# Residues of weights and block sums in the seven-product jobs of a hybrid decoder block on one core

## The chip, the cores and the metric

The kernel runs on one core of one Trainium2 chip. The metric is the device time of one execution in microseconds (us); where several executions are timed, their median. One execution is also recorded by the hardware profiler; its trace gives the start and the length of every instruction.

## What is computed

One decoder block on x of shape (1, 256, 2048), all in float32:

```
h = rms_norm(x);  z = h @ w_in                       # 2048 x 11280, split into p, q, k, v, g, r, gates
y_a = pool_mixer(p) @ w_branch_a                      # trailing-window means
o   = gated linear attention(q, k, v, g), rms_norm, * silu(r)
y_b = o @ w_branch_b
x   = x + rms_norm((sig(g0) * y_a + sig(g1) * y_b) @ w_out)
h   = rms_norm(x)
x   = x + rms_norm((silu(h @ w_ffn_gate) * (h @ w_ffn_up)) @ w_ffn_down)   # 5632 wide
```

Nearly all work is in the products with w_in, w_branch_a, w_branch_b, w_out, w_ffn_gate, w_ffn_up and w_ffn_down: 256 rows of activations against weights that are read once.

## The kernel before, in words

**Precision.** Each float32 operand is held as a high part in TensorE's round float32 type and a low part that is the rest. A product is three matmuls: high activations by high weights, high by low, low by high. For weights, ScalarE writes the high part `wh` and VectorE the low part `wl` (lines 340 and 344, 407 and 411); for activations the tiles are called h0h, h0l and so on.

**Jobs.** The plan (a generator at the top) cuts the weights into jobs of 512 columns. A job's weights come in steps of two blocks of 128 rows (class `Step`): 12 matmuls of 512 columns (lines 371 to 373), weights streaming, activations (128 columns) loaded as the stationary operand. The first jobs (kinds p, q, k) run across: there the weights are stationary and the activations stream, 256 columns (lines 360 to 362).

**The seven products.** 46 jobs are marked fast. Their first eight row blocks are done as a 2 by 2 block product with seven multiplications in place of eight (class `Part`: q1, r5, q6, q7, q2, q4, r3). Each product is 4 row blocks x 3 matmuls = 12 matmuls of 256 columns (lines 431 to 433), weights streaming again. In r5, q7, q6 and r3 the activations are sums or differences of blocks, made once for an activation by `combine` and kept in tiles `x`, `fx` (for the three parts of the FFN product) or `ox` (for o). In q1, q2 and q4 they are blocks of the whole activations. The other row blocks of a fast job are steps: four steps in a job with 16 row blocks, two in one with 12.

**Order.** Jobs are merged by `merged`: in the long run of a product TensorE sees, job after job, q2, a step, q4, q1 of the next job, r3, r5 of the next, a step, q6, a step, q7, a step. Transposes for the next operand (line 203) are put between units by `to_operand` and others. Weights are prepared four units ahead (`prepare_to`), so DMAs, ScalarE and VectorE work ahead of TensorE.

**Where tiles lie.** Each tile has a byte address in every partition. Modulo 256, summed from the tile sizes in order of the pools and the pads of 64 (pool `his`) and 192 bytes (pool `wp`): whole activations, high and low, 0; weights `wh` and `wl` of steps and of the seven products alike, 64, in slots of 4352 = 17 x 256 bytes; block sums `x` 128 (a slot at 0 and AT_X = 128); block sums `fx` 128 (a slot at 64 and AT_F = 64); block sums `ox` 0; raw weights 192 or 64 in turn; blocks of raw weights for the seven products, 64. All steps inside these tiles are multiples of 256 bytes. The text calls the residue of the streaming operand less that of the stationary one, modulo 256, the **relation** of a matmul. It is 64 for steps and for q1, q2, q4; 64 for all seven in the w_branch_b jobs; 192 in r5, q7, q6 and r3 of the others. In the jobs that run across it is 0 - 64 = 192.

Of the kernel before, what the change touches and what calls it, by code (L numbers as in the profile page):

```python
# [8 lines left out]
F32 = mybir.dt.float32  # L9
# [5 lines left out]
P = 128  # L15
# [14 lines left out]
HW = CW // 2  # L30
# [4 lines left out]


LINE = 256
PAD_A, PAD_B, PAD_W = 64, 0, 192
ROOM_W = 4352
AT_X, AT_F = 128, 64  # L40
ROOM_X = 8448
AHEAD = 12
SUMS_AHEAD = 7
# [9 lines left out]
COMBOS = ("r5", "q7", "q6", "r3")  # L53
# [55 lines left out]
def tile_hybrid_block(ctx: ExitStack, tc: tile.TileContext, *aps):  # L109
# [4 lines left out]
    act, dve, pool, pe, sync = nc.scalar, nc.vector, nc.gpsimd, nc.tensor, nc.sync  # L114

    one = ctx.enter_context(tc.tile_pool(name="one", bufs=1))
    his, st, los, rest = [ctx.enter_context(tc.tile_pool(name=n, bufs=b))
                          for n, b in (("his", 1), ("st", 4), ("los", 1), ("rest", 1))]
    wp = ctx.enter_context(tc.tile_pool(name="wp", bufs=BUFS))
# [7 lines left out]
    late = {}  # L127

    def placed(pool, shape, tag, name, lead=0, room=0):

        n = 1
        for k in shape:
            n *= k
        t = pool.tile([P, max(room // 4, n)], F32R, tag=tag, name=name)[:, lead // 4:lead // 4 + n]
        if len(shape) == 2:
            return t.rearrange("p (a b) -> p a b", a=shape[0])
        return t.rearrange("p (a b c) -> p a b c", a=shape[0], b=shape[1])
# [3 lines left out]
    def nm(s):  # L141
        uid[0] += 1
        return f"{s}_{uid[0]}"
# [10 lines left out]
    def f32(ap):  # L154
        return ap.bitcast(F32)


    for p_, n in ((his, PAD_A), (los, PAD_B), (wp, PAD_W)):
        if n:
            p_.tile([P, n // 4], F32, tag="pad", name=nm("pad"), bufs=1)  # L160
    xa = [one.tile([P, D], F32, tag=f"X{t}", name=f"x{t}") for t in range(NT)]
    ident = one.tile([P, P], F32, tag="ident", name="ident")
    masks = two_st.tile([P, 64 * MASKED + P], I32, tag="masks", name="masks")
# [48 lines left out]
    def extra(a):  # L212


        if a.name == "o":
            k = [two_st.tile([P, 2, 4, P], F32R, tag=f"K{i}", name=nm("ox")) for i in range(2)]
            q = [[two_st.tile([P, 4, P], F32R, tag=f"{x}{i}", name=nm("ox")) for i in range(2)] for x in ("Q", "AD")]
            return [tuple(x) for x in q] + [(x[:, 0], x[:, 1]) for x in k]
        if a.name[0] == "f":
            if not late:  # L220
                early.close()
                late["pool"] = ctx.enter_context(tc.tile_pool(name="late", bufs=1, reuse_waits="tile"))
            x = [placed(late["pool"], (len(COMBOS), 4, P), f"fx{i}", nm("fx"), AT_F, ROOM_X) for i in range(2)]
        else:
            x = [placed(pool_, (len(COMBOS), 4, P), f"R{i}", nm("x"), AT_X, ROOM_X) for i, pool_ in enumerate((his, rest))]
        return [(x[0][:, n], x[1][:, n]) for n in range(len(COMBOS))]

    class Act:
# [16 lines left out]
        def combine(self):  # L245

            self.x = {}
            parts = {}
            pieces = extra(self)

            def block(name, g, t):
                parts[name] = scratch().rearrange("p (k c) -> p k c", k=4)
                c = (slice(None), slice(None), slice(t * P, (t + 1) * P))
                dve.tensor_tensor(parts[name], f32(self.hi[g][c]), f32(self.lo[g][c]), op=ALU.add)

            def put(which, name):
                n, src = COMBOS.index(which), parts.pop(name)
                hi, lo = pieces[n]
                act.activation(hi, src, AF.Copy)
                dve.tensor_tensor(lo, src, f32(hi), op=ALU.subtract)  # L260
                self.x[which] = (hi, lo)
                parts[which] = src

            def differ(dst, a, b, op=ALU.subtract):
                dve.tensor_tensor(parts[dst], parts[a], parts[b], op=op)

            return [lambda: (block("21", 0, 1), block("22", 1, 1)),
                    lambda: (differ("22", "21", "22"), put("r5", "22")),
                    lambda: (block("11", 0, 0), differ("21", "11", "21")),
                    lambda: (put("q7", "21"), differ("11", "r5", "11")),  # L270
                    lambda: (put("q6", "11"), block("12", 1, 0)),
                    lambda: (differ("12", "12", "q6", ALU.add), put("r3", "12"))]
# [47 lines left out]
    class Step:  # L320
# [16 lines left out]
        def high(self):  # L337
            self.load()
            self.hi = placed(wp, (GK, self.j.width), "wh", nm("wh"), room=ROOM_W)
            act.activation(self.hi, self.raw, AF.Copy)  # L340

        def low(self):
            self.lo = placed(wp, (GK, self.j.width), "wl", nm("wl"), room=ROOM_W)
            dve.tensor_tensor(self.lo, self.raw, f32(self.hi), op=ALU.subtract)  # L344
# [32 lines left out]
    class Part:  # L377
# [25 lines left out]
                pool.dma_start(self.block((0, 1)), self.block((0, 0)), accum_op=ALU.add)  # L403

        def high(self):
            self.hi = placed(wp, (4, HW), "wh", nm("wh"), room=ROOM_W)
            act.activation(self.hi, self.src, AF.Copy)  # L407

        def low(self):
            self.lo = placed(wp, (4, HW), "wl", nm("wl"), room=ROOM_W)  # L410
            dve.tensor_tensor(self.lo, self.src, f32(self.hi), op=ALU.subtract)  # L411

        def left(self, i):
# [689 lines left out]
```

## Time and profile before

| | |
|---|---|
| median of 3 runs | 1479.87 us (1478.96 to 1480.27) |
| profiled execution, its own time | 1477.55 us |
| span from its first to its last instruction | 1475.7 us |
| TensorE matmul busy | 1454.2 us, 99% |
| VectorE busy | 1219.9 us, 83% |
| ScalarE busy | 907.6 us, 62% |
| granted TensorE clock, mean | 0.999 |

In a timeline row the first number is the start in us from the span's start, the second the length of the instruction. Matmuls overlap (a new one starts while the one before still drains), so a matmul's length says little; the pace is the difference between the starts of two successive ones, and the time of a unit of 12 matmuls is the start of the next unit less its own.

### The profile page before, as it was taken

How to read it: one execution, taken by the hardware profiler on the slowest of the kernel's cores; microseconds unless marked ns; L12 is line 12 of the kernel's file. 1: busy time of each engine (PE TensorE's matmuls, PEld its weight loads, DVE VectorE, ACT ScalarE, POOL GpSimd, SP SyncE). 2: the span in 40 equal slices, each digit the busy share in tenths (PEclk: the TensorE clock that was granted, in tenths of full speed). 3: DMA queues.
4: the chain of work that ended last, by engine and by line, in shares of the span. 5: the costliest groups of instructions: out<-in, count | busy, mean ns of one | idle time of the engine just before them, and what ended most of it. 6: DMA issues, size and time to landing. Idle time of an engine off the chain costs nothing.

```text
span 1475.7 us, 23511 instructions
## 1 busy us (share of the span) xinstructions
PE 1454.2 (99%) x9156; PEld 1299.3 (88%) x9156; DVE 1219.9 (83%) x1359; ACT 907.6 (62%) x1185; POOL 73.0 (5%) x96
## 2 busy tenths in 40 slices
PE   8999999999999999999999999999999999999997
PEld 7988999888888888889878988998998899998886
DVE  6765445789899897799778899888889899889997
ACT  6457433556676665556666666666666666666663
POOL 2000000000110000000000000000000000000001
PEclk9999999999999999999999999999999999999999
DMA  8857765435668688658855677777766777777654
GB/s 286 272 179 230 216 188 182 129 100 184 229 188 258 191 255 259 208 169 283 259 186 158 214 225 220 228 227 230 245 216 212 228 231 228 228 237 229 202 176 144
DMA packets 88896, 314.70 MB, mean 213 GB/s; under 512 B 10140, under 2 KB 10352, under 8 KB 88528
## 3 DMA queue, kind: packets, MB, share of 16 engines
q1 hardware_dynamic: 77616, 279.15, 56.4%
q0 software_dynamic: 8160, 28.59, 10.2%
q10 hardware_dynamic: 3008, 5.45, 1.0%
q8 instruction: 72, 1.18, 0.3%
q14 instruction: 40, 0.33, 0.1%
HBM read 284.84 MB, written 4.19 MB: 196 GB/s over the span
## 4 chain that ended last, share of the span: by engine, by line
PE 85%; DVE 6%; issue 3%; DMA 3%; ACT 2%; POOL 0%; SPq 0%; DVEq 0%; ACTq 0%; POOLq 0%
PE acc L372 15%; PE acc L373 15%; PE acc L371 15%; PE ac L432 5%; PE ac L431 5%; PE ac L433 5%; PE acc L433 4%; PE acc L432 4%; PE acc L431 4%; PE acc L362 3%; PE acc L360 3%; PE acc L361 3%; DVE wl L411 2%; DVE wl L344 2%; PE tr L685 1%
## 5 line engine op out<-in xcount | busy, mean ns | idle before, releaser
L340 ACT ACTIVATE wh<-raw 128x1024 fp32r<-128x1024 f32 (+1 forms) x336 | 355.3, 1059 | 303.3 <-PE acc L373 129.8
L344 DVE TENSOR_TENSOR wl<-raw,wh 128x1024 fp32r<-128x1024 f32 (+1 forms) x336 | 410.5, 1223 | 130.5 <-ACT wh L340 128.0
L411 DVE TENSOR_TENSOR wl<-blocks,wh 128x1024 fp32r<-128x1024 f32 x322 | 390.8, 1222 | 71.6 <-ACT wh L407 69.7
L407 ACT ACTIVATE wh<-blocks 128x1024 fp32r<-128x1024 f32 x322 | 338.5, 1059 | 158.3 <-PE acc L373 65.7
L431 PE MATMUL ac<-wh,x 128*128 128x256 f32 x396 | 110.4, 279 | 0.0
L432 PE MATMUL ac<-wl,x 128*128 128x256 f32 x396 | 109.9, 278 | 0.0
L433 PE MATMUL ac<-wh,x 128*128 128x256 f32 x396 | 109.8, 277 | 0.0
L403 POOL DMA_DIRECT2D blocks<-blocks x46 | 39.9, 867 | 812.9 <-DVE wl L344 209.5
L431 PEld LDWEIGHTS ac<-wh,x 128*128 128x128 f32 x396 | 74.5, 188 | 2.9
L432 PEld LDWEIGHTS ac<-wl,x 128*128 128x128 f32 x396 | 74.4, 188 | 3.1
L433 PEld LDWEIGHTS ac<-wh,x 128*128 128x128 f32 x396 | 74.4, 188 | 0.0
L372 PE MATMUL acc<-wl,h22h 128*128 128x512 f32 x176 | 69.6, 395 | 0.2
L371 PE MATMUL acc<-wh,h22h 128*128 128x512 f32 x176 | 69.4, 394 | 0.2 <-ACT wh L340 0.2
L373 PE MATMUL acc<-wh,h23l 128*128 128x512 f32 x176 | 69.3, 394 | 0.0
L373 PE MATMUL acc<-wh,h22l 128*128 128x512 f32 x176 | 69.2, 394 | 0.0
L372 PE MATMUL acc<-wl,h23h 128*128 128x512 f32 x176 | 69.1, 392 | 0.0
L371 PE MATMUL acc<-wh,h23h 128*128 128x512 f32 x176 | 68.4, 390 | 0.5 <-ACT wh L340 0.5
L396 DVE TENSOR_TENSOR blocks<-blocks,blocks 128x1024 f32<-128x1024 f32 x46 | 56.3, 1223 | 1.3
L392 DVE TENSOR_TENSOR blocks<-blocks,blocks 128x1024 f32<-128x1024 f32 x46 | 56.2, 1221 | 0.7
L394 DVE TENSOR_TENSOR blocks<-blocks 128x1024 f32<-128x1024 f32 x46 | 56.1, 1219 | 0.1
L371 PE MATMUL acc<-wh,h3h 128*128 128x512 f32 (+1 forms) x128 | 49.6, 387 | 0.0
L372 PE MATMUL acc<-wl,h3h 128*128 128x512 f32 (+1 forms) x128 | 49.5, 387 | 0.0
(536 smaller groups left out, 4096.9 us busy)
## 6 DMA issues: line engine op xcount, KB each, us to landing
raw<-in_w_in_dram SPq DMA_DIRECT2D x128, 512.0 KB, 4.1
raw<-in_w_ffn_gate_dram SPq DMA_DIRECT2D x48, 512.0 KB, 4.4
raw<-in_w_ffn_up_dram SPq DMA_DIRECT2D x48, 512.0 KB, 4.4
blocks<-blocks POOLq DMA_DIRECT2D x46, 512.0 KB, 6.1
blocks<-in_w_ffn_down_dram SPq DMA_DIRECT2D x44, 512.0 KB, 4.3
raw<-in_w_ffn_down_dram SPq DMA_DIRECT2D x44, 512.0 KB, 4.4
blocks<-in_w_in_dram SPq DMA_DIRECT2D x40, 512.0 KB, 4.5
blocks<-in_w_ffn_gate_dram SPq DMA_DIRECT2D x40, 512.0 KB, 4.3
```

Source lines behind the costliest of these rows:

```text
L340: act.activation(self.hi, self.raw, AF.Copy)
L344: dve.tensor_tensor(self.lo, self.raw, f32(self.hi), op=ALU.subtract)
L371: pe.matmul(ps, ah, hi[:, i, cs], start=first, stop=False, skip_group_check=j.fast)
L372: pe.matmul(ps, ah, lo[:, i, cs], start=False, stop=False, skip_group_check=j.fast)
L373: pe.matmul(ps, al, hi[:, i, cs], start=False, stop=last, skip_group_check=j.fast)
L392: dve.tensor_tensor(b12, b12, b22, op=ALU.add)
L396: dve.tensor_tensor(b21, b21, b12, op=ALU.add)
L407: act.activation(self.hi, self.src, AF.Copy)
L411: dve.tensor_tensor(self.lo, self.src, f32(self.hi), op=ALU.subtract)
L431: pe.matmul(dst, ah, wh, start=i == 0 and p in ("q1", "r5"), stop=False, skip_group_check=True)
L432: pe.matmul(dst, ah, wl, start=False, stop=False, skip_group_check=True)
L433: pe.matmul(dst, al, wh, start=False, stop=i == 3 and p in EARLY, skip_group_check=True)
```

## The change

The slots and their sizes stay; what lies in them is shifted. The weights of the seven products start 128 bytes further into their slots (residue 192 in place of 64), those of steps stay at 64. The block sums `x` start at their slot's begin (residue 0 in place of 128), `fx` 192 bytes into it (0 in place of 128). `ox` stays at 0. A pad of zero bytes is dropped; it allocated nothing.

```diff
-PAD_A, PAD_B, PAD_W = 64, 0, 192
+PAD_A, PAD_W = 64, 192
 ROOM_W = 4352
-AT_X, AT_F = 128, 64
+LEAD_FAST = 128
+LEAD_F = 192
 ROOM_X = 8448
...
-            x = [placed(late["pool"], (len(COMBOS), 4, P), f"fx{i}", nm("fx"), AT_F, ROOM_X) for i in range(2)]
+            x = [placed(late["pool"], (len(COMBOS), 4, P), f"fx{i}", nm("fx"), LEAD_F, ROOM_X) for i in range(2)]
         else:
-            x = [placed(pool_, (len(COMBOS), 4, P), f"R{i}", nm("x"), AT_X, ROOM_X) for i, pool_ in enumerate((his, rest))]
+            x = [placed(pool_, (len(COMBOS), 4, P), f"R{i}", nm("x"), room=ROOM_X) for i, pool_ in enumerate((his, rest))]
...
         def high(self):
-            self.hi = placed(wp, (4, HW), "wh", nm("wh"), room=ROOM_W)
+            self.hi = placed(wp, (4, HW), "wh", nm("wh"), LEAD_FAST, ROOM_W)
             act.activation(self.hi, self.src, AF.Copy)
 
         def low(self):
-            self.lo = placed(wp, (4, HW), "wl", nm("wl"), room=ROOM_W)
+            self.lo = placed(wp, (4, HW), "wl", nm("wl"), LEAD_FAST, ROOM_W)
             dve.tensor_tensor(self.lo, self.src, f32(self.hi), op=ALU.subtract)
```

The relation becomes 192 in all seven products of every fast job and stays 64 in steps.

## Rows read from the trace of the kernel before

**Rows 1.** From the page: the span, TensorE's busy time, and its granted clock in 40 slices.

```profile
span 1475.7 us, 23511 instructions
PE 1454.2 (99%) x9156; PEld 1299.3 (88%) x9156; DVE 1219.9 (83%) x1359; ACT 907.6 (62%) x1185; POOL 73.0 (5%) x96
...
PEclk9999999999999999999999999999999999999999
```

**Rows 2.** The list of waits of TensorE over the whole span, longest total first (in total, times, longest); its first three.

```profile
PE tr L203 <- DMA x<-in_x_dram: 4.1, 6, 1.2
PE acc L372 <- DVE wl L344: 1.8, 2, 1.5
PE acc L371 <- ACT wh L340: 1.2, 3, 0.6
```

**Rows 3.** From the page's costliest groups: the four groups that write the weights of steps (lines 340, 344) and of the seven products (lines 407, 411); busy us, mean ns of one.

```profile
L340 ACT ACTIVATE wh<-raw 128x1024 fp32r<-128x1024 f32 (+1 forms) x336 | 355.3, 1059 | 303.3 <-PE acc L373 129.8
L344 DVE TENSOR_TENSOR wl<-raw,wh 128x1024 fp32r<-128x1024 f32 (+1 forms) x336 | 410.5, 1223 | 130.5 <-ACT wh L340 128.0
L411 DVE TENSOR_TENSOR wl<-blocks,wh 128x1024 fp32r<-128x1024 f32 x322 | 390.8, 1222 | 71.6 <-ACT wh L407 69.7
L407 ACT ACTIVATE wh<-blocks 128x1024 fp32r<-128x1024 f32 x322 | 338.5, 1059 | 158.3 <-PE acc L373 65.7
```

**Rows 4.** Timeline of TensorE from 924 to 937 us, first matmul of each unit of 12 (line 371 a step, line 431 one of the seven products).

```profile
924.58 0.39 PE L371 MATMUL acc<-wh,h22h 128*128 128x512 f32 x1
...
927.33 0.28 PE L431 MATMUL acc<-wh,h21h 128*128 128x256 f32 x1
...
928.69 0.28 PE L431 MATMUL ac<-wh,f00h 128*128 128x256 f32 x1
...
930.05 0.28 PE L431 MATMUL acc<-wh,x 128*128 128x256 f32 x1
...
932.77 0.39 PE L371 MATMUL acc<-wh,h22h 128*128 128x512 f32 x1
...
935.52 0.28 PE L431 MATMUL ac<-wh,fx 128*128 128x256 f32 x1
...
936.89 0.39 PE L371 MATMUL acc<-wh,h23h 128*128 128x512 f32 x1
```

**Rows 5.** Timeline of TensorE from 948 to 955 us: four transposes, then the first matmul of each unit.

```profile
948.48 0.60 PE L203 MATMUL tr<-ident,scr 128*128 128x128 f32 x4
948.83 0.36 PE L431 MATMUL acc<-wh,f01h 128*128 128x256 f32 x1
...
950.33 0.28 PE L431 MATMUL ac<-wh,f00h 128*128 128x256 f32 x1
...
951.74 0.28 PE L431 MATMUL acc<-wh,fx 128*128 128x256 f32 x1
...
953.12 0.28 PE L431 MATMUL ac<-wh,fx 128*128 128x256 f32 x1
...
954.48 0.39 PE L371 MATMUL acc<-wh,f02h 128*128 128x512 f32 x1
```

**Rows 6.** Timeline of TensorE from 822 to 843 us, first matmul of each unit.

```profile
822.88 0.28 PE L431 MATMUL ac<-wh,h20h 128*128 128x256 f32 x1
...
824.29 0.28 PE L431 MATMUL acc<-wh,x 128*128 128x256 f32 x1
...
825.71 0.28 PE L431 MATMUL ac<-wh,x 128*128 128x256 f32 x1
...
827.12 0.40 PE L371 MATMUL acc<-wh,h22h 128*128 128x512 f32 x1
...
829.93 0.28 PE L431 MATMUL ac<-wh,x 128*128 128x256 f32 x1
...
831.34 0.40 PE L371 MATMUL acc<-wh,h23h 128*128 128x512 f32 x1
...
834.15 0.28 PE L431 MATMUL ac<-wh,x 128*128 128x256 f32 x1
...
838.36 0.28 PE L431 MATMUL acc<-wh,h21h 128*128 128x256 f32 x1
...
839.78 0.40 PE L371 MATMUL acc<-wh,h22h 128*128 128x512 f32 x1
...
842.54 0.28 PE L431 MATMUL acc<-wh,h21h 128*128 128x256 f32 x1
```

**Rows 7.** Busy time of TensorE by stretch, 158 to 247 us, when nothing but matmuls of jobs that run across is on it (length, busy and, in brackets, the number of matmuls; then the granted clock).

```profile
158.00:247.00 89.00, 89.00 (x758) 1.00 0.65 197
```

**Rows 8.** Timeline of TensorE: the first and the last of the 81 products among the 322 whose matmuls ran at 117 to 119 ns from start to start, each by its second and its fourth group of three (the last is followed by the step behind it).

```profile
330.08 0.28 PE L431 MATMUL ac<-wh,h0h 128*128 128x256 f32 x1
...
330.79 0.28 PE L431 MATMUL ac<-wh,h0h 128*128 128x256 f32 x1
...
1440.67 0.28 PE L431 MATMUL acc<-wh,f21h 128*128 128x256 f32 x1
...
1441.38 0.28 PE L431 MATMUL acc<-wh,f21h 128*128 128x256 f32 x1
...
1441.73 0.40 PE L371 MATMUL acc<-wh,f22h 128*128 128x512 f32 x1
```

**Rows 9.** Timeline of TensorE: the second and the third product after the transposes at 863.68 us, first matmul of each.

```profile
865.48 0.28 PE L431 MATMUL ac<-wh,h20h 128*128 128x256 f32 x1
...
866.84 0.28 PE L431 MATMUL acc<-wh,x 128*128 128x256 f32 x1
```

More of the change, by code (lines that the diff above doesn't have):

```diff
@@ L155, in f32 @@
         return ap.bitcast(F32)
-    for p_, n in ((his, PAD_A), (los, PAD_B), (wp, PAD_W)):
-        if n:
-            p_.tile([P, n // 4], F32, tag="pad", name=nm("pad"), bufs=1)
+    for p_, n in ((his, PAD_A), (wp, PAD_W)):
+        p_.tile([P, n // 4], F32, tag="pad", name=nm("pad"), bufs=1)
     xa = [one.tile([P, D], F32, tag=f"X{t}", name=f"x{t}") for t in range(NT)]
```

## The prediction

> **What bounds the kernel now.** I read the page's first two parts, then the waits of TensorE, then the timeline unit by unit. TensorE is busy for 1454.2 of 1475.7 us, and every slice of the span shows the granted clock at its upper level, 2.4 GHz [rows 1]. Its three longest waits add up to 7.1 us [rows 2]. So TensorE is the bound nearly everywhere, and only two things can move the end: the number of matmuls, which the change leaves as it is, and the pace at which one matmul follows another.
>
> The pace is where the reader has to look closely, because lengths of matmuls hide it. A product of 12 matmuls of 256 columns takes 1.36 us from its first start to the next unit's (927.33 to 928.69), that is 113 ns a matmul; a step takes 2.75 us (924.58 to 927.33) [rows 4]. But the same product can take more. After four transposes the products at 948.83 and 950.33 take 1.50 and 1.41 us, and the next two, on block sums, 1.38 and 1.36 [rows 5]. In [rows 6] products take 1.41 or 1.42 us one after the other, steps between them 2.81 us (827.12 to 829.93 and 831.34 to 834.15), and the quick pace is back only at 842.54. Clock and operands are alike in both. I read this as **two paces** of the same matmuls: 113 ns (quick) and 118 ns (slow, 0.71 us for six in [rows 8]). Going through all 322 products in this way, 81 ran slow, the first at 329.62 and the last at 1440.32 us; [rows 8] shows both at that pace.
>
> Three things about the paces matter for the change.
> - Transposes between units tend to leave the slow pace behind [rows 5], though not always: in [rows 9] the product after such a set is quick, 1.36 us.
> - With a constant relation of the two operands the slow pace does not heal. In the jobs that run across, 758 matmuls fill 89 us, 117 ns each, without a return to 113 [rows 7].
> - With a change of relation it may heal. In [rows 5] the slow pace ends where products on whole activations (relation 64) give way to products on block sums (relation 192); in [rows 6], at 824.29, the same change does nothing. Counted over the timeline in the same way, this meeting of a slow product of relation 64 with one of 192 occurs 15 times: 9 heal (one in [rows 5]), 6 do not (one in [rows 6]).
>
> **The change, part by part.**
>
> *Removed and added instructions:* none. No DMA, no wait and no queue is touched, and slots keep their sizes, so no other tile moves.
>
> *Writers of the shifted tiles.* ScalarE needs 1059 ns for a `wh`, whether it reads raw weights at residue 192 or 64 or blocks at 64; VectorE needs 1223 and 1222 ns for a `wl` in the two cases [rows 3]. No row shows a `wh` at 192, but source residues that differ by 128 make no difference here, so I take 0. Should each write cost 10 ns more, 322 of them would be 3 us per engine, and both engines idle far longer than that in front of these lines, waiting for others [rows 3]; what covers them is TensorE's own length. In this part the range gets nothing.
>
> *Products on block sums (r5, q7, q6, r3).* Both operands move by 128, the relation stays at 192. If only the relation counts, their own pace is unchanged.
>
> *Products on whole activations (q1, q2, q4, and all seven on `ox`).* Their relation goes from 64 to 192. Both relations run at 113 ns when quick: 1.36 us for the whole ones at 927.33 and 928.69, 1.36 us each for the two on block sums from 930.05 to 932.77 [rows 4]. So the steady quick pace costs 0.
>
> *Entry behind a step.* A product that keeps the step's relation takes 1.36 us behind it (927.33), one that changes it takes 1.37 us (935.52 to 936.89) [rows 4]: 0.01 us. There are 83 products of relation 64 straight behind a step in the trace, and all change their relation now: 83 x 0.01 = **+0.8 us**. From below, if a shift of the streaming operand is free where one of the loaded operand was not, the 84 entries that pay today pay nothing: -0.8 us.
>
> *Healing.* This is the large term. The order behind a set of transposes is q4, q1, r3, r5, step, q6, step, q7, step. Today the relation changes between q1 and r3, two products after the transposes. Afterwards it is 192 for all four, and changes only at steps (192 to 64 and back). That is the pattern of [rows 6] from 824.29 on, where products at 192 and steps at 64 alternate and both stay slow over four products and three steps; the pace is quick again only after a product of relation 64 has had its turn, at 842.54. No such product is left after the change. Prices: 1.41 - 1.36 = 0.05 us a product, 2.805 - 2.75 = 0.055 us a step.
>
> How much of the kernel would that catch, if a slow pace once set held until the next set of transposes that leaves a quick one? From 812 us on, eight sets leave it slow (821, 907, 949, 1115, 1158, 1200, 1324, 1407 us) and three quick (864, 1073, 1367). Between a slow one and the next quick one lie 2 + 8 + 12 + 3 = 25 jobs: 175 products, of which 35 are slow already, 140 x 0.05 = 7.0 us; 100 steps, of which 4 are slow already, 96 x 0.055 = 5.3 us. Before 812 us, the stretches 456 to 617 and 684 to 770 us hold about 53 quick products and 36 quick steps that follow a slow spell: 2.7 + 2.0 us. Together **17.0 us** at full persistence. From below the term can be negative: if the new residues prevent the slow pace, all of today's goes, 81 x 0.05 + 16 x 0.055 = 4.9 us.
>
> Between these ends I take the share in which a change of relation failed to heal, 6 of 15: 0.4 x 17.0 = **+6.8 us**.
>
> *Sum:* +0.8 + 6.8 = +7.6 us. Against the profiled execution, 1477.55 us, that gives 1485.2 us. That execution lies 2.3 us under the median of the runs shown; on the median, 1479.87 us, the forecast is **1487.5 us**.
>
> A rule that speaks against any effect: the same step and the same product have two times in the rows above, and the relation changes at places where the pace changes. The Trainium skill, "TensorE: Matmul & The Clock Gate", section "Step-by-step: what each phase is for", says that TensorE reads SBUF through two independent ports, so that loading the next stationary operand takes nothing from the running matmul. By it residues would be of no account and the sum 0 us.
>
> **The rivals.**
> - *B, healing at steps.* The slow pace ends at the first step behind the transposes, since the relation now changes there, so two more products per slow set are slow: 14 sets x 2 x 0.05 = 1.4 us, with the entries at most +2.2 us, at least about 0: 1480 to 1482 us, centre 1481. For it: 9 of 15 changes of relation healed. Against it: in [rows 6] three steps healed nothing. Residues without any effect, the case of the cited rule, give the same within 0.2%.
> - *C, the other side: no slow pace left.* Its place is the first product behind a set of transposes. If weights at 192 against activations at 0 fall into the quick pace there, as one set in [rows 9] did with weights at 64, nothing sets the slow pace and 4.9 us go: 1475.0 us. It decides if more than 3 of the 4.9 us go, that is if about 6 in 10 slow spells vanish. Against it: the jobs that run across stay slow at this very relation [rows 7].
> - *D, slow throughout.* 241 quick products and 162 quick steps of fast jobs turn slow: 12.1 + 8.9 = 21 us, 1501 us. Against it: some sets leave the quick pace [rows 9], and [rows 4] shows quick alternation of 192 and 64.
>
> **How the numbers follow.** The forecast case (slow pace that outlives most steps) has 0.41; its own range is 1482.9 to 1497.7 us, from a fifth of the persistence term to all of it. B has 0.31, C 0.24, D 0.04. The predicted time is the forecast's, 1487.5 us. The range must reach to B and C: 1475.0 to 1496.0 us leaves out D, the uppermost end of the forecast and the part of C that gains all. A change of 0.2%, 3 us, is about what a measurement of this kernel can tell. Faster by more: most of C, 0.22. Slower by more: the forecast and D, 0.45. Within: B and the rest of C, 0.33.
>
> **What would show it.** In the changed kernel's timeline, behind transposes such as those before 948.83, q4, q1, r3 and r5 should take 1.41 us each, the step behind them 2.81 and not 2.75, and q6 again 1.41; a set that leaves the quick pace should give 1.36 us up to the next transposes. Every product straight behind a step should take 1.37 us or more. Writers of weights should keep 1059 and 1222 ns, waits of TensorE their few us. Rival B shows as 2.75 us in the first step behind a slow set, rival C as 1.36 us in the second product behind most sets. The forecast is wrong if the slow products number about 81 again, or if the quick pace itself is no longer 113 ns.

## The result, and the profile after

The changed kernel's median is 1485.71 us (1483.37 to 1486.76, 6 runs), that of the kernel before on the same chip 1479.41 us (1475.85 to 1480.27, 6 runs). The ratio is 1.0048, with a 95% interval of 1.0038 to 1.0058: slower by 6 to 7 us, where 7.6 were forecast (1487.5 us). The way to it is another one than forecast.

From the page of the changed kernel: span, TensorE's busy time, granted clock, and the two groups that write the shifted weights (busy us, mean ns of one). They answer to [rows 1, 3].

```profile
span 1483.7 us, 23511 instructions
PE 1463.9 (99%) x9156; PEld 1307.8 (88%) x9156; DVE 1220.3 (82%) x1359; ACT 906.9 (61%) x1185; POOL 72.9 (5%) x96
...
PEclk9999999999999999999999999999999999999999
...
L411 DVE TENSOR_TENSOR wl<-blocks,wh 128x1024 fp32r<-128x1024 f32 x322 | 391.1, 1221 | 74.8 <-ACT wh L407 70.9
...
L407 ACT ACTIVATE wh<-blocks 128x1024 fp32r<-128x1024 f32 x322 | 337.9, 1057 | 157.2 <-PE acc L373 62.7
```

The span is 8.0 us longer and TensorE is busy 9.7 us longer, with as many matmuls and the clock at its upper level in every slice. The writers take 1221 and 1057 ns, against 1222 and 1059 before. TensorE's waits, as in [rows 2] (total, times, longest):

```profile
PE tr L203 <- DMA x<-in_x_dram: 3.1, 5, 1.2
PE acc L372 <- DVE wl L344: 1.8, 3, 1.0
```

They are no longer than before, so the 8 us lie in the pace of the matmuls. The next view is the timeline of TensorE in the changed kernel from 865 to 879 us: four transposes, then the first matmul of each unit (of the first step also the second triple). It answers to [rows 5, 9].

```profile
865.64 0.60 PE L203 MATMUL tr<-ident,scr 128*128 128x128 f32 x4
866.00 0.37 PE L431 MATMUL acc<-wh,h21h 128*128 128x256 f32 x1
...
867.45 0.28 PE L431 MATMUL ac<-wh,h20h 128*128 128x256 f32 x1
...
868.81 0.28 PE L431 MATMUL acc<-wh,x 128*128 128x256 f32 x1
...
870.17 0.28 PE L431 MATMUL ac<-wh,x 128*128 128x256 f32 x1
...
871.53 0.40 PE L371 MATMUL acc<-wh,h22h 128*128 128x512 f32 x1
...
872.23 0.39 PE L371 MATMUL acc<-wh,h22h 128*128 128x512 f32 x1
...
874.29 0.28 PE L431 MATMUL ac<-wh,x 128*128 128x256 f32 x1
...
875.70 0.40 PE L371 MATMUL acc<-wh,h23h 128*128 128x512 f32 x1
...
878.46 0.28 PE L431 MATMUL ac<-wh,x 128*128 128x256 f32 x1
```

Read the differences of the starts. Behind the transposes q4 takes 1.45 us (0.20 us of it between its first two matmuls), and q1, r3 and r5 take 1.36 us each: the quick pace, where [rows 5] had 1.50 and 1.41 for the first two. Then comes a step, 871.53 to 874.29, and the product behind it is slow: 874.29 to 875.70, 1.41 us. The step behind that one takes 2.76 us, not the 2.81 of a slow one. Of the 11 sets of transposes from 812 us on, 6 leave the quick pace like this one (3 before); in the other 5 the first two products are slow, in 4 of them all four, and the first undisturbed step behind those is quick all the same, as at 956.91 (2.76 us), with a slow product behind it (1.42 us):

```profile
955.50 0.28 PE L431 MATMUL ac<-wh,fx 128*128 128x256 f32 x1
...
956.91 0.40 PE L371 MATMUL acc<-wh,f02h 128*128 128x512 f32 x1
...
959.67 0.28 PE L431 MATMUL ac<-wh,fx 128*128 128x256 f32 x1
...
961.09 0.40 PE L371 MATMUL acc<-wh,f03h 128*128 128x512 f32 x1
```

**What the transposes leave no longer matters much: the products' pace is lost at every step, and the steps themselves stay quick.**

Counted in the starts over the whole trace, 268 of 322 products are slow (81 before). Of the 167 products straight behind a step, 166 are slow. Before, 67 of the 83 at relation 64 (whole activations, and six on `ox`) and 70 of the 84 on the other block sums were quick there.

Where the 8 us lie, worked out over all starts of matmuls, from the first to the last:

| spacings between starts of matmuls | before, us | after, us | difference |
|---|---|---|---|
| in products, undisturbed (3833 spacings in either trace) | 439.73 | 448.38 | +8.65 |
| in products, with a stall or transposes | 9.44 | 8.62 | -0.82 |
| in steps, from 325 us on, undisturbed | 636.59 | 638.57 | +1.98 |
| in steps, with a stall | 25.59 | 24.50 | -1.09 |
| in jobs that run across, and the rest | | | -0.75 |
| sum | | | +7.97 |

187 more slow products x 0.05 us make 9.4 us. Before, 70 quick products on block sums paid 0.01 us each behind a step; that is gone, which takes 0.7 us back and gives the 8.65. Steps take 2 us more in sum: a step behind a product takes 2.763 us in the mean, against 2.754 before, when 16 steps of 2.80 us were among them and the others took 2.748. Its first triple now needs 0.70 us (871.53 to 872.23), then it runs as before. The 16 slow steps of before all stand straight behind slow products at 64/128, as in [rows 6]; the change leaves no product with these residues, and but for one step the pace of 2.80 us is gone.

### The profile page after: what moved, and what is told of

It is laid out like the page before. It is cut to its first block, busy times and chain, and to the rows that moved or that the text cites. A ratio compares the mean times of both kernels' runs of the same rounds, so it can differ in the third digit from the quotient of the medians.

```text
span 1483.7 us, 23511 instructions
## 1 busy us (share of the span) xinstructions
PE 1463.9 (99%) x9156; PEld 1307.8 (88%) x9156; DVE 1220.3 (82%) x1359; ACT 906.9 (61%) x1185; POOL 72.9 (5%) x96
## 4 chain that ended last, share of the span: by engine, by line
PE 87%; DVE 5%; issue 3%; DMA 2%; ACT 1%; POOL 0%; SPq 0%; DVEq 0%; ACTq 0%; POOLq 0%
PE acc L371 16%; PE acc L373 15%; PE acc L372 15%; PE ac L431 5%; PE ac L432 5%; PE ac L433 5%; PE acc L431 4%; PE acc L433 4%; PE acc L432 4%; PE acc L362 3%; PE acc L360 3%; PE acc L361 3%; DMA raw<-in_w_in_dram 2%; DVE wl L344 2%; PE tr L685 1%
## 5 line engine op out<-in xcount | busy, mean ns | idle before, releaser
L340 ACT ACTIVATE wh<-raw 128x1024 fp32r<-128x1024 f32 (+1 forms) x336 | 355.1, 1059 | 309.9 <-PE acc L373 130.6
L411 DVE TENSOR_TENSOR wl<-blocks,wh 128x1024 fp32r<-128x1024 f32 x322 | 391.1, 1221 | 74.8 <-ACT wh L407 70.9
L407 ACT ACTIVATE wh<-blocks 128x1024 fp32r<-128x1024 f32 x322 | 337.9, 1057 | 157.2 <-PE acc L373 62.7
L392 DVE TENSOR_TENSOR blocks<-blocks,blocks 128x1024 f32<-128x1024 f32 x46 | 56.2, 1222 | 0.9
L371 PE MATMUL acc<-wh,h2h 128*128 128x512 f32 (+1 forms) x128 | 49.6, 388 | 0.0
```

The source lines that it names most:

```text
L371: pe.matmul(ps, ah, hi[:, i, cs], start=first, stop=False, skip_group_check=j.fast)
L392: dve.tensor_tensor(b12, b12, b22, op=ALU.add)
```

## The experiments

Every experiment keeps instructions, queues, slots and order; only residues differ, always by a multiple of 128 bytes from one of the two kernels. The lines of code are cuts, in 1 to 8 against the changed kernel, in 9 and 10 against the one before. Ratios are against the kernel before on the same chip. "192/0" is a matmul with streaming operand (weights) at residue 192 and stationary one (activations) at 0. "Behind a step" counts products that follow a step directly and undisturbed.

**1. The sums moved alone.** Sums at 0, weights all at 64: every relation is 64.

```diff
-LEAD_FAST = 128
+LEAD_FAST = 0
```

> Half of the change: block sums at residue 0, weights of the products back at 64, so the relation is 64 everywhere and neither operand's residue moves between a step and a product. Theory M (the streaming operand's residue moves from 64 to 192 at the border from a step to a product, and that sets the slow pace): no border is left, so products straight behind a quick step are quick, 1.36 us; slow ones come from transposes alone. Between 60 and 200 slow products of 322, 1476 to 1486 us. Theory R (weights at 192 over activations at 0 are slow behind any step): the same, under 100 slow products, about 1477 us. Theory K (the prediction's: transposes set the slow pace, only a change of relation can heal it): no change of relation is left, over 250 slow products, about 1488 us.

Measured: 1480.32 us, ratio 1.0033 (1.002 to 1.0045); 220 products slow. Timeline of its TensorE, first matmul of each unit:

```profile
869.16 0.39 PE L371 MATMUL acc<-wh,h22h 128*128 128x512 f32 x1
...
871.90 0.28 PE L431 MATMUL ac<-wh,x 128*128 128x256 f32 x1
...
873.32 0.39 PE L371 MATMUL acc<-wh,h23h 128*128 128x512 f32 x1
...
876.06 0.28 PE L431 MATMUL ac<-wh,x 128*128 128x256 f32 x1
```

A slow product (1.42 us) stands between two steps of 2.74 us. With one relation everywhere the slow pace of products lives through quick steps: 60 of 167 products behind steps are quick. This part of the change alone costs 0.33% of the time, the whole change 0.48%. The count lies outside what each of the three theories expected.

**2. The weights moved alone.** Products 192/0 and 192/128.

```diff
-LEAD_F = 192
+LEAD_F = 64
...
-            x = [placed(pool_, (len(COMBOS), 4, P), f"R{i}", nm("x"), room=ROOM_X) ...
+            x = [placed(pool_, (len(COMBOS), 4, P), f"R{i}", nm("x"), 128, ROOM_X) ...
```

> The other half: weights of the products at 192, block sums at 128 as before. The relation is then 64 in the products on block sums, as in steps, and 192 in those on whole activations. Theory M: the streaming operand moves at every border, so nearly all products behind a step are slow, about 268 slow ones, 1486 us as with the whole change. A theory by relation alone (only a change from 64 to 192 at the border counts): of the products behind steps, those on block sums (q6, q7, about half) are quick, 1.36 us, and 120 to 180 are slow, about 1482 us. Theory K: about 81 to 180 slow, 1480 to 1484 us.

Measured: 1481.23 us, 1.0037 (1.0025 to 1.005); 184 slow. Its timeline:

```profile
875.71 0.28 PE L431 MATMUL ac<-wh,x 128*128 128x256 f32 x1
...
877.07 0.40 PE L371 MATMUL acc<-wh,h23h 128*128 128x512 f32 x1
...
879.83 0.28 PE L431 MATMUL acc<-wh,h21h 128*128 128x256 f32 x1
...
881.24 0.40 PE L371 MATMUL acc<-wh,h22h 128*128 128x512 f32 x1
```

The same kernel, both products behind a step of 64/0: on block sums (192/128) 1.36 us, on whole activations (192/0) 1.41 us. Over the trace 81 of 84 of the former are quick and 0 of 83 of the latter. This is the clearest run against my main reading: 192/0 has the very relation, 192, that 64/128 had before the change, where 70 of 84 were quick behind the same steps. So the relation alone does not decide the pace of a product, although the expectation by relation alone comes nearest to this run's counts; both residues count.

**3. All weights at 192**, those of steps too (same two lines as in the change, in class Step: lines 339 and 343).

```diff
-            self.hi = placed(wp, (GK, self.j.width), "wh", nm("wh"), room=ROOM_W)
+            self.hi = placed(wp, (GK, self.j.width), "wh", nm("wh"), LEAD_FAST, ROOM_W)
```

> The change, and the weights of steps moved by 128 bytes too: all weights at 192, all activations at 0, relation 192 everywhere, no border. Theory M: as with the sums moved alone, since nothing moves between step and product: between 60 and 200 slow products, 1476 to 1486 us. Theory R: all products behind steps slow, 260 or more, 1486 us or more. Theory K: constant relation, over 250 slow, about 1488 us.

Measured: 1486.88 us, 1.0077 (1.0063 to 1.0091); only 76 slow. Its timeline:

```profile
873.95 0.28 PE L431 MATMUL ac<-wh,x 128*128 128x256 f32 x1
...
875.31 0.39 PE L371 MATMUL acc<-wh,h22h 128*128 128x512 f32 x1
...
878.10 0.28 PE L431 MATMUL ac<-wh,x 128*128 128x256 f32 x1
...
879.47 0.39 PE L371 MATMUL acc<-wh,h23h 128*128 128x512 f32 x1
```

Products are quick again, 1.36 and 1.37 us (137 of 167 behind steps), now that products and steps lie alike. The time goes to the steps: 2.79 us (875.31 to 878.10), in every undisturbed step from 325 us on. Their undisturbed spacings, counted as in the table above, make 646.7 us against 636.6 before: +10.2 us of the 10.8 measured. Lines 339 and 343 also place the weights of the jobs that run across, whose relation goes from 192 to 64; their matmuls keep 117 ns (117.2 in the mean before, 117.5 here). The count is what theory M expected, the time is not.

**4. The mirror**: steps at 192, products at 64, activations and sums at 0 (experiment 3, with 0 for LEAD_FAST in lines 406 and 410).

> The border mirrored: weights of steps at 192, weights of products at 64, all activations at 0. Theory M: the streaming operand moves by 128 at each border as in the change, only the other way, modulo 256 the same: about 268 slow products, 1486 us. If the direction counts, the products behind steps are quick and the time is 1475 to 1478 us. Theory R: products at 64 over 0, quick behind steps as in the kernel before, under 100 slow, about 1477 us.

Measured: 1495.59 us, 1.0135 (1.0121 to 1.0149), the slowest of all; 317 slow, 1 of 167 quick behind steps. Its timeline:

```profile
875.48 0.28 PE L431 MATMUL ac<-wh,x 128*128 128x256 f32 x1
...
876.90 0.39 PE L371 MATMUL acc<-wh,h22h 128*128 128x512 f32 x1
...
879.69 0.28 PE L431 MATMUL ac<-wh,x 128*128 128x256 f32 x1
```

Products 1.42 us, steps 2.79: here weights that move by 128 bytes between a step and a product over unmoved activations make the product slow from the other side as well, as 64/0 to 192/0 did in the change. None of the three expectations had a time near this.

**5. The kernel before with the products' weights 256 bytes further** (LEAD_FAST = 256, sums at 128 as before).

> The kernel before with the weights of the products 256 bytes further into their slots (residue modulo 256 as before, 64; sums at 128). If residues count modulo 256, nothing changes: about 81 slow products of 322, ratio 0.998 to 1.002. If what counts is that the streaming operand lies elsewhere in its slot, or a modulus of 512 or more, the products straight behind steps turn slow as with 128 bytes: 180 or more slow ones, ratio 1.003 or more.

Measured: 1476.35 us (11 runs), 0.9996 (0.9986 to 1.0005). A whole 256 bytes do nothing that can be told from no change; half of it, over the same sums, gave 1.0037 (experiment 2). So residues modulo 256 count. Its profiled execution had 110 slow products (61 of 83 and 62 of 84 quick behind steps), that of the kernel before 81. I take this for a variation between executions, whose times go from 1474.0 to 1480.0 us for the kernel before on this chip alone; with one trace of each kernel it isn't shown.

**6. The activations moved in place of the weights**: all weights 64, all activations and sums 128 (`ox` 0).

```diff
-PAD_A, PAD_W = 64, 192
+PAD_A, PAD_W = 192, 64
...
-LEAD_FAST = 128
-LEAD_F = 192
+LEAD_FAST = 0
+LEAD_F = 64
```

> All weights at 64 as before, all activations and block sums at 128 (pads changed; only the sums for w_branch_b stay at 0): relation 192 everywhere, reached from the other side than with all weights at 192. If the pace of a step goes by the relation, steps take 2.80 us as they did there and products are mostly quick (under 110 slow): ratio 1.006 to 1.009. If it goes by where the weights lie (64 quick, 192 slow), steps take 2.75 us, and the ratio is 0.997 to 1.004 depending on what transposes leave.

Measured: 1485.87 us, 1.0063 (1.005 to 1.0076); 48 slow. Its timeline:

```profile
872.87 0.28 PE L431 MATMUL ac<-wh,x 128*128 128x256 f32 x1
...
874.23 0.39 PE L371 MATMUL acc<-wh,h22h 128*128 128x512 f32 x1
...
877.02 0.28 PE L431 MATMUL ac<-wh,x 128*128 128x256 f32 x1
```

The picture of experiment 3, and what was expected if a step goes by the relation: quick products (154 of 161 behind steps), steps of 2.79 us. Steps at 64/128 and at 192/0 share nothing but the relation 192; those at 64/0 take 2.75. So for **steps** the relation does count: 0.05 us each between 64 and 192, as far as these three pairs of residues tell; relation 64 was run in steps as 64/0 alone.

**7. Sums and their weights only**: sums' products 192/128, whole ones left at 64/0.

```diff
-            self.hi = placed(wp, (4, HW), "wh", nm("wh"), LEAD_FAST, ROOM_W)
+            self.hi = placed(wp, (4, HW), "wh", nm("wh"), LEAD_FAST * (self.part in COMBOS), ROOM_W)
```

> Products on block sums with weights at 192 and sums at 128, products on whole activations with weights at 64 over 0, steps at 64 over 0: relation 64 everywhere, though both operands move by 128 at the border of a product on sums. Theory S (a relation changed by the streaming operand at the border sets the slow pace; both moved together or nothing moved does not): q6 and q7 behind steps quick, 1.36 us, q2 and q4 quick unless transposes left the slow pace; 60 to 140 slow products, ratio 0.999 to 1.003. If any movement of the streaming operand at a border sets the slow pace, q6 and q7 are slow: 180 or more, ratio 1.004 or more.

Measured: 1483.20 us, 1.0044 (1.0029 to 1.0058); 237 slow. A miss. Its timeline:

```profile
877.78 0.28 PE L431 MATMUL ac<-wh,x 128*128 128x256 f32 x1
...
879.14 0.40 PE L371 MATMUL acc<-wh,h23h 128*128 128x512 f32 x1
...
881.90 0.28 PE L431 MATMUL acc<-wh,h21h 128*128 128x256 f32 x1
...
883.31 0.40 PE L371 MATMUL acc<-wh,h22h 128*128 128x512 f32 x1
```

The sums' products are quick behind steps (80 of 84; 877.78, 1.36 us). The whole ones, which lie exactly as before the change and whose steps do too, are slow: 1 of 77 quick (881.90, 1.41 us). So the step hands on something of the products *before* it.

**8. The mirror with sums at 128**: experiment 3 with the sums of experiment 2; all weights 192, sums' products 192/128.

> All weights at 192, whole activations at 0 (steps, q1, q2, q4: relation 192), block sums at 128 (r5, q7, q6, r3: relation 64): the border of the sums' products is mirrored, and it is the loaded operand that moves. Theory S: these products stay quick behind steps, as in the kernel before, though their relation changes; under 120 slow products, steps 2.80 us as with all weights at 192, ratio 1.006 to 1.009. If any change of relation from 192 to 64 sets the slow pace (as when it was done with the weights, 317 slow), over 180 slow products, ratio 1.010 to 1.014.

Measured: 1490.25 us, 1.0095 (1.008 to 1.011); 133 slow. Its timeline:

```profile
875.08 0.28 PE L431 MATMUL ac<-wh,x 128*128 128x256 f32 x1
...
876.44 0.39 PE L371 MATMUL acc<-wh,h22h 128*128 128x512 f32 x1
...
879.23 0.28 PE L431 MATMUL ac<-wh,x 128*128 128x256 f32 x1
...
880.64 0.40 PE L371 MATMUL acc<-wh,h23h 128*128 128x512 f32 x1
```

The product ahead of the step is quick (1.36 us), that behind it slow (1.41), with the same two residues. Behind steps 82 of 83 products at 192/0 are quick and 0 of 84 at 192/128. My theory by then, that a shift of the loaded operand alone does no harm, falls.

**What orders the runs so far.** The three matmuls of a triple (high by high, high by low, low by high) are not spaced alike. In nanoseconds, the spacings of a quick step are 226, 229 and 232, in this order in the kernel before, and as 232, 226, 229 in the changed one: the long spacing lies behind the third matmul there, behind the first here. I call its place the step's **phase**. It is below what the 0.01 us of the rows show, so I counted it in the starts, over the six kernels so far that have steps at 64/0. The table leaves out 51 of their 1002 products behind steps, nearly all of them behind steps at 2.80 us, where few are quick:

| phase of the step ahead (long spacing behind) | products behind it that are quick |
|---|---|
| the third matmul | 64/0: 189 of 189; 64/128: 128 of 128; 192/0: 0 of 3; 192/128: 0 of 2 |
| the first | 64/0: 0 of 126; 192/0: 0 of 249; 64/128: 4 of 4; 192/128: 160 of 160 |
| the second | 0 of 90 |

Quick products with weights at 64 leave the step in the first of these phases, those with weights at 192 in the second. Slow products with weights at 64 leave it in any of the three. So the weights' residue of a quick product goes with the phase of the step behind it, and the phase with both residues of the next product goes with that one's pace; that the one sets the other is my reading of these counts. In the changed kernel nearly all fall into the cell 192/0 with "the first": 0 of 249 over these kernels. This table was found after the fact; the next two runs were made to try it.

**9. A turn behind the transposes.** The kernel before, but in 14 jobs, those behind most sets of transposes, the four products between transposes and first step (q4, q1 of the next job, r3, r5) get weights at 192. By the table, a quick spell should then come through the step.

```diff
...
+    tags = [(kind, n) for kind, n, *_ in plan()]
+    for i, j in enumerate(jobs[:-1]):
+        if j.fast and (tags[i] in (("v", 1), ("v", 2), ("v", 3), ("gates", 0)) or tags[i - 1][0] == "up" and tags[i] != ("down", (2, 0))):
+            for w in [w for w, _ in j.units] + jobs[i + 1].early:
+                if w.part in (("q4", "r3") if w.j is j else ("q1", "r5")):
+                    w.lead = 128
```

> The kernel before, except that in the 14 jobs where transposes stand ahead of q4 (after v1 to v3 and gates0 have begun, and after each up job but the last) the four products behind them, q4, q1, r3, r5, have their weights at 192. By the table of the runs so far: products with weights at 192 over 0 are quick behind transposes in 10 of 14 such places in the changed kernel, against 3 with weights at 64; products at 192 over 128 keep a quick pace; they leave the step in the phase whose longest spacing is ahead of the high-by-low matmul, in which a product at 64 over 128 was quick 4 times of 4. Expected: 20 to 50 slow products instead of 81, under 6 steps at 2.80 us, ratio 0.997 to 0.9995. If a step left in that phase makes the next products slow whatever their residues (the theory that any movement of the streaming operand at a border does harm), 110 or more slow, ratio 1.001 or more.

Measured: 1474.48 us, 0.9971 (0.996 to 0.9982): faster than both kernels; 41 slow products and 3 undisturbed slow steps in its profiled execution, against 81 and 16, as expected. Its timeline at the place of [rows 5]:

```profile
946.11 0.60 PE L203 MATMUL tr<-ident,scr 128*128 128x128 f32 x4
946.46 0.37 PE L431 MATMUL acc<-wh,f01h 128*128 128x256 f32 x1
...
947.92 0.28 PE L431 MATMUL ac<-wh,f00h 128*128 128x256 f32 x1
...
949.28 0.28 PE L431 MATMUL acc<-wh,fx 128*128 128x256 f32 x1
...
950.64 0.28 PE L431 MATMUL ac<-wh,fx 128*128 128x256 f32 x1
...
952.00 0.40 PE L371 MATMUL acc<-wh,f02h 128*128 128x512 f32 x1
...
954.76 0.28 PE L431 MATMUL ac<-wh,fx 128*128 128x256 f32 x1
...
956.13 0.39 PE L371 MATMUL acc<-wh,f03h 128*128 128x512 f32 x1
```

The four products take 1.46, 1.36, 1.36 and 1.36 us, where [rows 5] has 1.50, 1.41, 1.38 and 1.36, and the product behind the step (64/128) is quick, 1.37 us. Over the trace, 17 of 17 at 64/128 are quick behind a step of the phase "the first", a cell that had only 4 cases. But 11 of the quick products at 64/128 leave their step in this phase again, so the weights' residue is not all that sets it. The undisturbed spacings of products are 2.0 us less in sum than before and those of steps 0.8 us, 2.8 of the 3.1 us between the two profiled executions. That the medians differ by 4.9 us I can't split up, since only one execution of each has a trace.

**10. The whole ones' weights alone**: the kernel before with whole products at 192/0, sums left at 64/128.

```diff
-            self.hi = placed(wp, (4, HW), "wh", nm("wh"), room=ROOM_W)
+            self.hi = placed(wp, (4, HW), "wh", nm("wh"), 128 * (self.part not in COMBOS), room=ROOM_W)
```

> Products on whole activations with weights at 192 over 0, products on block sums as before with weights at 64 over 128: relation 192 in all seven, as in the change, but reached by the two operands in turn. By the table (pace behind a step goes by the step's phase and both residues): q2 and q4 slow behind nearly every step (75 or more of 83), q6 and q7 quick behind nearly every step (75 or more of 84); 110 to 190 slow products in all, ratio 1.001 to 1.004. By the relation alone it is the change again: about 268 slow, q6 and q7 slow, ratio 1.0048.

Measured: 1489.88 us, 1.0072 (1.0058 to 1.0085); 238 slow products and 139 undisturbed slow steps. It is slower than either theory had it, and the expectation by the table failed: behind steps 6 of 84 products on sums were quick, where 75 or more were expected, and 45 of 82 others slow, where 75 or more were expected. Its timeline:

```profile
868.10 0.37 PE L431 MATMUL acc<-wh,h21h 128*128 128x256 f32 x1
...
869.55 0.28 PE L431 MATMUL ac<-wh,h20h 128*128 128x256 f32 x1
...
870.91 0.28 PE L431 MATMUL acc<-wh,x 128*128 128x256 f32 x1
...
872.33 0.28 PE L431 MATMUL ac<-wh,x 128*128 128x256 f32 x1
...
873.75 0.40 PE L371 MATMUL acc<-wh,h22h 128*128 128x512 f32 x1
```

The two 192/0 products behind transposes that start at 867.74 are quick (869.55, 1.36 us), and the pace falls from one product to the next, with no step between, at 870.91 (1.42 us), where 64/128 follows 192/0; this happens 15 times. The step table says nothing of such places. From there slow products on sums put 113 steps into the pace of 2.80 us. The 57 products behind steps at the quick pace fall as the table has it. The other 110 stand behind slow steps, which the table leaves out: all 37 at 192/0 are quick there, none of the 73 at 64/128. The table describes quick steps at 64/0 and could not foresee how many steps would be slow.

## Why the prediction was right in size and wrong in its way

- **The bound: right.** TensorE bounds the kernel, and only its pace changed; writers and waits are as they were, as costed.
- **The steady quick pace at relation 192: right.** 192/0 runs at 1.36 us where it is quick (866 to 871 us), so that term is 0.
- **The entry, +0.8 us: wrong in kind.** It presumed that a product which changes the relation behind a step stays quick and pays 0.01 us. Of 167, one stayed quick. The cost of these places is 0.05 us each, the whole loss of the pace.
- **The healing, +6.8 us: the size nearly right, the mechanism wrong.** The step that failed was "a slow pace once set by transposes holds". The four products behind transposes at 1.41 us came in 4 of 11 sets; but the step behind them took 2.76 us there (956.91 to 959.67) and not 2.81, and a quick set did not hold up to the next transposes either: its first step ended it. The 0.4 from 6 of 15 meetings has nothing to do with what happened. The term was 0.4 x (7.0 + 2.7) = 3.9 us for products and 0.4 x (5.3 + 2.0) = 2.9 us for slow steps. Measured were +8.65 us for the undisturbed spacings of products (entries among them) and +1.98 us for those of steps, at 2.763 us a step. The products, 0.8 + 3.9 us in the forecast, were undersized by nearly half, the steps were forecast too dear, and 2.7 us less in stalls and across jobs, which no term foresaw, brought the sum back to 8.0 us. That the sum fits is luck. The slow steps of [rows 6], from which 2.805 us was taken, stand behind products at 64/128, which the change removes.
- **"If only the relation counts": wrong for products, right for steps as far as they were run.** Experiment 2 shows the first, 3 and 6 with their 2.79 us the second. It was the premise under both terms, and [rows 4] held a warning that I passed over: the 0.01 us of extra time at 935.52 already showed that what stands ahead of a product counts.
- **Rivals.** B (healing at the first step) is turned round: steps do the harm. C named the first product behind transposes as the place that decides; 192/0 did fall into the quick pace there in 6 of 11 sets, and it availed nothing beyond the next step. What spoke against C was no evidence: jobs that run across keep 117 ns at relation 64 as well (117.5 to 117.8 in experiments 3, 4, 6 and 8). D (all slow, 1501 us) comes nearest to the count of slow products, 268, and took slow steps to be part of it; they are not, but for a few.
- **The rule on ports.** By the Trainium skill, "TensorE: Matmul & The Clock Gate", section "Step-by-step: what each phase is for", loading the stationary operand takes nothing from the running matmul. The prediction concluded from it that residues are of no account and the sum is 0. These runs disagree with that conclusion: the same 23511 instructions with operands moved by 128 bytes take from 0.9971 to 1.0135 of the time before. Whether the two ports hinder each other, no run here shows.

What stays open: why a triple has phases at all, why 192/0 keeps no pace behind one phase and 192/128 does, and the falls inside a row of products in experiment 10. The table rests on counts; of its two forward tests one was met (9) and one failed (10), though behind quick steps its cells held there too. No run separates TensorE's own two reads from what other engines and DMAs read and write at the same time, and none shows the cause inside the engine.

## What to carry to other kernels

Where a streak of matmuls is the bound, read the differences between starts, unit by unit, and look whether the same unit has two times; then look at what stands ahead of the slow one and where both operands lie modulo 256. A residue is to be chosen for a whole sequence, not for one product: moving the sums or the weights alone gave 1.0033 and 1.0037, moving both 1.0048 (the intervals overlap), and the fastest version turns the weights only where a quick spell has to be started. A forecast that comes out near the measured time proves nothing of its steps: the count of slow units told at once that the mechanism was another.

## What the runs showed of the hardware

- Matmuls of 256 columns go at 113 or 118 ns from start to start at the same granted clock, and which one depends on the residues modulo 256 of both operands and on the matmuls ahead. A shift of weights by 256 bytes does nothing that can be told (0.9996); shifts by 128 gave 0.9971 to 1.0135.
- Matmuls of 512 columns in steps go at 229 ns (2.75 us a step) at 64/0 and at 233 ns (2.79 us) at relation 192, by weights at 192 (experiment 3) or activations at 128 (experiment 6); but a step at relation 64 can run at 2.80 us too, behind slow products on sums at 64/128 (experiment 10, and 16 times in the kernel before).
- The product's pace and the step's go separate ways: in experiment 1 slow products stand between quick steps, in experiment 6 quick ones between slow steps.
